# Column sums of two norms as one sum of two blocks, split into high and low parts, against one sum in fp32 of each block

## The chip, the core and the metric

The kernel runs on one core of one Trainium2 chip. Four engines compute: TensorE (PE) multiplies matrices, and its weight loads are listed as PEld; VectorE (DVE) and ScalarE (ACT) work element by element; GpSimd (POOL) and SyncE (SP) issue most of the transfers here. Every engine works through its own queue in order. SBUF holds 128 partitions; matrix products arrive in PSUM banks of 128 x 512 floats. The metric is the time of one execution on the device, in microseconds (us); lower is better.

## The reference: one step of a two-layer decoder

1024 prompt tokens and 8 sample tokens of width 2048 pass through layer A (an input projection, causal pooling over windows of 2 to 16 tokens, a linear map for each group, a SiLU gate, an output projection), then through layer B (sliding-window attention over a key and value computed once, a gate, an output projection). After each layer stands the same residual and norm:

```python
def layer_norm(x, g, b):
    xf = x.astype(jnp.float32)
    mu = jnp.mean(xf, axis=-1, keepdims=True)
    var = jnp.mean(jnp.square(xf - mu), axis=-1, keepdims=True)
    return ((xf - mu) * lax.rsqrt(var + LN_EPS) * g.astype(jnp.float32) + b.astype(jnp.float32)).astype(x.dtype)
...
    return layer_norm(ALPHA * x + y, g_ln, b_ln), new_state
```

All inputs and outputs are fp32.

## The kernel before

**Tiles.** Activations lie with the 2048 channels on the partitions: 16 tiles of 128 channels, handled two at a time as eight pairs p = 0..7, and the tokens along the row. The tokens come in two chunks: c = 0 with 512, and c = 1 with 520 (512 prompt tokens and the 8 samples). Most SBUF memory is a pool of 53 buffers of 128 x 1040 floats (`Mem`); `full()` takes a buffer, `half()` half of one, and what was freed longest ago is taken first.

**Products.** To hold fp32 accuracy in the faster form fp32r, every operand is split: ScalarE casts the high part (L473 for weights, L751 for activations), VectorE subtracts it from the whole to get the low part (L488, L760), and each product becomes three matmuls, high x high, high x low, low x high (L640 to L642, or L668 to L670 in the plain phases). Most projections go by Strassen's seven products of half blocks (`seven`, `pair`, `both`); PSUM is emptied by ScalarE and VectorE (L581 to L613).

**Steps.** The program is written out step by step: `begin()` loads, casts and splits weights some steps ahead (`ahead`), then 24 matmuls are issued, then `end()` raises the step counter `i` and issues what was put there with `at(n, go)` (n steps later) or, for TensorE, with `product(n, rank, go)`. Work beside the products is written as Python generators; `end()` advances the first of them one turn (up to its next `yield`) in every `every`-th step, if enough buffers are free. `in_order` then fixes the source order on TensorE, VectorE and ScalarE. The phases are ai (input projection A), ao (output projection A), bi and bo (the same of layer B), each for c = 0 and then c = 1.

**Norms.** A sum over channels is a sum over partitions and tiles. Pairs are first added up on VectorE into one buffer `acc` of two blocks (128 x 2 x T); the two blocks are then multiplied by J, a 128 x 128 matrix of 1/2048, which sums the partitions and puts the mean on each of them. That is `j_sum`: two fp32 matmuls that add up in one PSUM bank, for 520 tokens in two halves of 260 (L845). It is called
- in `shifted` (L1203), in the output phases of c = 0 (ao, bo) and in the last phase, bo of c = 1: the sum of the first pair gives a shift that is subtracted from every pair (L1217), so that the sums of squares (L1223, L1229) stay small. The step order for the first pair is: sum one step after, subtraction, squares and addition two, three and four steps after;
- in `ln_gen` (L864), a generator: the mean (L886), then for c = 0 the variance from the collected squares (L913), for c = 1 from squares of the centred values (L900; L914); then 1/sqrt (`rstd`, L856 to L859); then pair by pair the subtraction of the mean (L935), the multiplication (L936), scale and shift on ScalarE (L927) and the transfer out. `quiet()` yields until the PSUM bank of these sums (`psO`) has been unused for a step.

`ln_gen` runs three times: layer A, c = 0 during ao of c = 1 (a turn every second step); layer A, c = 1 during the first, plain part of bi of c = 0, with the transform of h behind it (`t_gen`); layer B, c = 0 during bo of c = 1 (a turn every third step; the rest is run out after the last product). The 520 tokens of layer B are normed by `phase_end`, which ends the program and has its own fp32 sums (L1291, L1367), untouched by the change. There the last three pairs are worked off with `less` (L1267), `rest` (L1273), `square` (L1278), `add` (L1281, L1282), `affine` (L1309, L1310, L1317), `scale` (L1329), then `moments` (L1383 to L1393) and the closing transposes and products (L1412, L1401, L1420) and evictions (L1432, L1437).

Of the kernel before, what the change touches and what calls it, by code (L numbers as in the profile page):

```python
# [10 lines left out]
F32R = mybir.dt.float32r  # L11
# [5 lines left out]
P = 128  # L17
D = 2048
NK = D // P
# [13 lines left out]
TMAX = 520  # L33
# [13 lines left out]
K_ID, K_MP, K_J, K_RC = 0, 128, 256, 384  # L47
# [134 lines left out]
class Kern:  # L182
    def __init__(self, ctx, tc, io):
        self.tc, self.io = tc, io
        self.nc = tc.nc
        pool = lambda name, **kw: ctx.enter_context(tc.tile_pool(name=name, **kw))
        one = pool("one", bufs=1)
        self.smp = pool("smp", bufs=2)
        dram = pool("dram", bufs=1, space=bass.MemoryType.DRAM)
        self.psd = [pool(f"psd{i}", bufs=1, space=bass.MemoryType.PSUM) for i in range(3)]  # L190
        self.pso = pool("pso", bufs=1, space=bass.MemoryType.PSUM)
        self.four = None
        ctx.callback(self.use_four, None)
        self.prm = one.tile([P, N_PRM], F32, name="prm")
        self.cst = one.tile([P, N_CST], F32, name="cst")
        self.mki = one.tile([P, P], I32, name="mki")
        self.nsink = one.tile([P, NH], F32, name="nsink")
        self.carry = one.tile([P, NK, NST], F32, name="carry")
        self.kdec = one.tile([P, 2, NDEC], F32, name="kdec")
        self.qd = [one.tile([P, NDEC, 8], F32, name=f"qd{i}") for i in range(2)]  # L200
        self.sgd = [one.tile([P, 8, NDEC], F32, name=f"sgd{i}") for i in range(2)]
        self.mem = Mem(pool("mem", bufs=1), NSLOT)
        self.n = 0
        self.i = self.e = self.lastO = self.turns = self.ring = 0
        self.posts, self.events, self.side = [], {}, []
# [12 lines left out]
        self.gbd = dram.tile([32, 2 * P], F32, tag="gbd", name="gbd")  # L218
        self.ws = {
            n: [dr(f"s{n}{q}", [P, 4, 1024]) for q in range(np_)]  # L220
            for n, np_ in (("wia", 16), ("woa", 8), ("wkv", 2), ("wib", 16), ("wob", 8))
        }
# [609 lines left out]
            yield  # L832


    def j_sum(self, T, src, out):

        J = self.cst[:, K_J : K_J + P]
        for s in [slice(0, T)] if T <= 512 else [slice(0, T // 2), slice(T // 2, T)]:
            n = s.stop - s.start
            if s.start == 0:  # L840
                ps = self.psO()[:, :n]
            else:
                ps = self.psW()[:, :n]
            for i, a in enumerate(src):
                self.nc.tensor.matmul(ps, J, a[:, s], start=i == 0, stop=i == len(src) - 1)  # L845
            out(s, ps)
# [17 lines left out]
    def ln_gen(self, c, pre, acc, gc, bc, out, td):  # L864
# [15 lines left out]
        flat = lambda s: s.a[:, : 2 * T]  # L880
        a2 = self.pair_view(acc, T)
        load(0)
        yield
        yield from self.quiet()
        load(1)
        self.j_sum(T, [a2[:, 0], a2[:, 1]], lambda s, ps: nc.scalar.copy(mu[:, s], ps))  # L886
        acc.free()
        yield
        w = self.mem.full()
        q, v = w.a[:, :T], w.a[:, TMAX : TMAX + T]  # L890
        if c == 0:
            sq = self.l_sq[0]
            nc.vector.tensor_mul(q, mu, mu)
        else:
            sq, sqs = self.mem.full(), {}
            for p in range(10):
                load(p + 2)
                if p < 8:
                    t = self.pair_view(pre[p], T)
                    nc.vector.tensor_sub(t, t, b2(mu))  # L900
                if 1 <= p <= 8:
                    sqs[p - 1] = sq if p == 1 else self.mem.full()
                    nc.scalar.activation(flat(sqs[p - 1]), flat(pre[p - 1]), AF.Square)
                yield
                if p > 2:
                    nc.vector.tensor_add(flat(sq), flat(sq), flat(sqs[p - 2]))
                    sqs[p - 2].free()
                yield
        s2 = self.pair_view(sq, T)
        yield from self.quiet()  # L910
        self.j_sum(
            T, [s2[:, 0], s2[:, 1]],
            lambda s, ps: nc.vector.scalar_tensor_tensor(v[:, s], ps, EPS, q[:, s], op0=ALU.add, op1=ALU.subtract)  # L913
            if c == 0 else nc.vector.tensor_scalar(v[:, s], ps, EPS, None, op0=ALU.add),  # L914
        )
        sq.free()
        yield
        self.rstd(v, rr, q)
        w.free()
# [283 lines left out]
    def shifted(self, c, p, s, pre, acc, end):  # L1203

        nc = self.nc
        T = CHUNKS[c][1]
        flat = lambda s: s.a[:, : 2 * T]
        box = {}

        def mean():  # L1210
            self.l_sq[c], self.l_sh[c] = self.mem.full(), self.mem.half()
            t = self.pair_view(s, T)
            self.j_sum(T, [t[:, 0], t[:, 1]], lambda h, ps: nc.scalar.mul(self.l_sh[c].a[:, h], ps, NK / 2.0))

        def less():
            t = self.pair_view(s, T)
            nc.vector.tensor_sub(t, t, self.l_sh[c].a[:, None, :T].to_broadcast([P, 2, T]))  # L1217
            if p >= KEEP0:
                nc.gpsimd.dma_start(self.act["p", c][:, 2 * p : 2 * p + 2, :], t)

        def square():
            q = box["q"] = self.l_sq[c] if p == 0 else self.mem.full()
            nc.scalar.activation(flat(q), flat(s), AF.Square)  # L1223

        def add():
            if p == 0:
                return
            nc.vector.tensor_add(flat(acc), flat(pre[0] if p == 1 else acc), flat(s))
            nc.vector.tensor_add(flat(self.l_sq[c]), flat(self.l_sq[c]), flat(box["q"]))  # L1229
            box["q"].free()  # L1230
            if p >= KEEP0:
                s.free(True)
            if p == 7:
                self.l_sh[c].free()

        if p == 0:
            pre.append(s)
            self.product(1, 1, mean)
        for n, go in zip((2, 3, 4) if p == 0 else (0, 1, 2), (less, square, add)):
            self.at(n, go)  # L1240

    def phase_end(self, c, xs, x_in, pre, acc, gc, bc, out):
# [761 lines left out]
    def start(self):  # L2004
# [19 lines left out]
        for j in range(4):  # L2024
            self.at(3 + 3 * j, lambda j=j: self.t_first(j))
        self.at(13, lambda: setattr(self, "x0", None))
        nc.vector.tensor_scalar(
            self.nsink[:], self.prm[:, C_SINK : C_SINK + NH], -1.0, None, op0=ALU.mult
        )
# [231 lines left out]
```

## Time and profile before

| | us |
|---|---|
| median of 3 runs | 2372.48 |
| lowest, highest | 2372.2, 2375.47 |
| the profiled execution | 2371.61 |
| its span, first to last instruction | 2369.8 |
| mean granted TensorE clock | 0.997 |

A row of the groups reads: line, engine, operation, output <- inputs (buffer numbers left out), shape, count | busy time, mean ns of one | idle time of the engine just before, and what ended it. In a timeline a row starts with its start and its duration in us; `x4` are four equal instructions in a row, and the bracket at the end is the idle time before it and what released it. TensorE's durations are longer than the distance from one start to the next, since matmuls are pipelined. An fp32 matmul leaves two records.

### The profile page before, as it was taken

How to read it: one execution, taken by the hardware profiler on the slowest of the kernel's cores; microseconds unless marked ns; L12 is line 12 of the kernel's file. 1: busy time of each engine (PE TensorE's matmuls, PEld its weight loads, DVE VectorE, ACT ScalarE, POOL GpSimd, SP SyncE). 2: the span in 40 equal slices, each digit the busy share in tenths (PEclk: the TensorE clock that was granted, in tenths of full speed). 3: DMA queues.
4: the chain of work that ended last, by engine and by line, in shares of the span. 5: the costliest groups of instructions: out<-in, count | busy, mean ns of one | idle time of the engine just before them, and what ended most of it. 6: DMA issues, size and time to landing. Idle time of an engine off the chain costs nothing. (4 is left out here: it accounts for less than half of the span.)

```text
span 2369.8 us, 46551 instructions
## 1 busy us (share of the span) xinstructions
PE 2335.5 (99%) x18444; PEld 2224.0 (94%) x18444; DVE 1914.7 (81%) x2369; ACT 1338.8 (56%) x2420; POOL 203.1 (9%) x379
## 2 busy tenths in 40 slices
PE   8999999999999999999999999999999999999998
PEld 6899999999999999998878899999999999999997
DVE  8787988776778878958988888887777768888787
ACT  4444446544546447644554666685666668546556
POOL 0111110011000000000111111100000000000001
PEclk9999999999999999999999999999999999999999
DMA  8678879989889979989888766788777768699785
GB/s 293 214 247 302 281 285 349 321 294 325 275 306 340 321 270 331 324 309 326 304 317 316 258 216 227 254 286 277 239 243 226 225 192 297 222 355 370 263 316 178
DMA packets 252059, 669.18 MB, mean 282 GB/s; under 512 B 25760, under 2 KB 106560, under 8 KB 251840
## 3 DMA queue, kind: packets, MB, share of 16 engines
q1 hardware_dynamic: 206368, 501.14, 63.2%
q0 software_dynamic: 45472, 165.07, 17.8%
q8 instruction: 144, 2.36, 0.4%
q14 instruction: 75, 0.61, 0.1%
HBM read 471.01 MB, written 185.59 MB: 277 GB/s over the span
## 5 line engine op out<-in xcount | busy, mean ns | idle before, releaser
L640 PE MATMUL pD<-m,m 128*128 128x260 f32 (+1 forms) x4752 | 1349.4, 284 | 9.8 <-DVE m L601 5.6
L642 PE MATMUL pD<-m,m 128*128 128x260 f32 (+1 forms) x4752 | 1340.8, 282 | 3.2 <-DVE m L488 3.2
L641 PE MATMUL pD<-m,m 128*128 128x260 f32 (+1 forms) x4752 | 1340.2, 282 | 0.0
L640 PEld LDWEIGHTS pD<-m,m 128*128 128x128 f32 x4752 | 896.0, 189 | 21.9 <-issue 12.9
L642 PEld LDWEIGHTS pD<-m,m 128*128 128x128 f32 x4752 | 896.7, 189 | 4.6 <-DVE m L488 4.4
L641 PEld LDWEIGHTS pD<-m,m 128*128 128x128 f32 x4752 | 896.6, 189 | 1.7 <-issue 1.4
L488 DVE TENSOR_TENSOR m<-m,m 128x1024 fp32r<-128x1024 f32 x674 | 814.5, 1219 | 101.7 <-ACT m L473 63.2
L473 ACT CAST m<-m 128x1024 fp32r<-128x1024 f32 x674 | 701.7, 1048 | 299.6 <-DVE m L331 72.6
L668 PE MATMUL pD<-m,m 128*128 128x512 f32 x448 | 179.7, 401 | 8.0 <-ACT m L751 8.0
L669 PE MATMUL pD<-m,m 128*128 128x512 f32 x448 | 177.2, 396 | 0.7 <-DVE m L760 0.7
L670 PE MATMUL pD<-m,m 128*128 128x512 f32 x448 | 177.2, 395 | 0.0
L760 DVE TENSOR_TENSOR m<-m,m 128x1024 fp32r<-128x1024 f32 (+1 forms) x120 | 147.0, 1226 | 6.6 <-ACT m L751 5.0
L613 ACT COPY m<-pD 128x260 f32<-128x260 f32 (+1 forms) x83 | 31.1, 375 | 195.2 <-PE pD L642 194.7
L751 ACT CAST m<-m 128x1024 fp32r<-128x1024 f32 (+1 forms) x120 | 125.8, 1052 | 13.6 <-PE pD L669 5.2
L331 DVE TENSOR_TENSOR m<-m,m 128x1024 f32<-128x1024 f32 x88 | 107.6, 1222 | 6.7 <-DMA m<-in_wia 3.8
L668 PEld LDWEIGHTS pD<-m,m 128*128 128x128 f32 x448 | 84.7, 189 | 29.9 <-ACT m L751 8.0
L601 DVE TENSOR_TENSOR m<-pD,m 128x260 f32<-128x260 f32 (+1 forms) x86 | 36.5, 424 | 85.7 <-PE pD L642 85.5
L669 PEld LDWEIGHTS pD<-m,m 128*128 128x128 f32 x448 | 84.7, 189 | 20.6 <-DVE m L760 1.8
L670 PEld LDWEIGHTS pD<-m,m 128*128 128x128 f32 x448 | 84.6, 189 | 19.7
L1729 ACT ACTIVATE m<-m,sm 128x128 f32<-128x128 f32 x256 | 99.4, 392 | 0.0
L1024 PE MATMUL pD<-m,m 128*128 128x260 f32 (+1 forms) x528 | 91.5, 323 | 0.0
L1024 PEld LDWEIGHTS pD<-m,m 128*128 128x128 f32 x528 | 79.5, 188 | 8.2
(235 smaller groups left out, 2125.0 us busy)
## 6 DMA issues: line engine op xcount, KB each, us to landing
m<-in_wia SPq DMA_DIRECT2D x124, 512.0 KB
m<-in_wib SPq DMA_DIRECT2D x120, 512.0 KB
swia<-m POOLq DMA_DIRECT2D x64, 512.0 KB, 4.6
m<-swia SPq DMA_DIRECT2D x64, 512.0 KB
m<-swoa SPq DMA_DIRECT2D x64, 512.0 KB
swib<-m POOLq DMA_DIRECT2D x64, 512.0 KB, 5.5
m<-swib SPq DMA_DIRECT2D x64, 512.0 KB
m<-swob SPq DMA_DIRECT2D x56, 512.0 KB
```

Source lines behind the costliest of these rows:

```text
L331: self.nc.vector.tensor_add(s[out].a[:, :1024], s[x].a[:, :1024], s[y].a[:, :1024])
L473: self.nc.scalar.copy(hi.r[:, :1024], self.stream[self.cast].src().a[:, :1024])
L488: self.nc.vector.tensor_sub(lo.r[:, :1024], s.src().a[:, :1024], hi.a[:, :1024])
L640: nc.tensor.matmul(ps[:, :TH], wh[:, s], h, start=new and k == 0, stop=False, skip_group_check=on)
L641: nc.tensor.matmul(ps[:, :TH], wh[:, s], l, start=False, stop=False, skip_group_check=on)
L642: nc.tensor.matmul(ps[:, :TH], wl[:, s], h, start=False, stop=k == 7, skip_group_check=on)
L668: nc.tensor.matmul(ps[:], wh[:, s], h, start=par == 0 and k == 0, stop=False)
L669: nc.tensor.matmul(ps[:], wh[:, s], l, start=False, stop=False)
L670: nc.tensor.matmul(ps[:], wl[:, s], h, start=False, stop=par == 1 and k == 7)
L751: self.nc.scalar.copy(h.r[:, :n], s.a[:, :n])
L760: self.nc.vector.tensor_sub(l.r[:, :n], s.a[:, :n], h.a[:, :n])
L1024: nc.tensor.matmul(ps[:, : cs.stop - cs.start], ws[:, s], d[:, cs], start=f0 and k == 0, stop=l0 and k == 3,)
```

## The change

`j_sum` is given one sum in two parts instead of two blocks. `j_steps` makes them in three steps: VectorE adds the two blocks (`add`), ScalarE casts the sum to fp32r (`high`), VectorE subtracts (`low`). J is cast to fp32r once, in the ninth step of the program (`jr`). The two matmuls of each sum are then fp32r. In `shifted` the three steps are put at the steps 0, 1 and 2 behind the first pair and the sum at 3 instead of 1; the work of the first two pairs moves two steps back. In `ln_gen` for c = 0 the three steps of the mean and of the variance are done together, in three turns at the start, where one yield stood; for c = 1 the three steps of the variance come one turn each ahead of its sum, and the mean stays as it was, in fp32 (`j_sum32`).

```diff
+        self.jr = one.tile([P, P], F32R, name="jr")
...
+    def j_steps(self, T, a, b, box, *free):
+
+        def add():
+            box["u"] = self.mem.half()
+            self.nc.vector.tensor_add(box["u"].a[:, :T], a, b)
+            for f in free:
+                f.free()
+
+        def high():
+            box["hl"] = self.mem.full()
+            self.nc.scalar.copy(box["hl"].r[:, :T], box["u"].a[:, :T])
+
+        def low():
+            u, hl = box.pop("u"), box["hl"]
+            self.nc.vector.tensor_sub(hl.r[:, TMAX : TMAX + T], u.a[:, :T], hl.a[:, :T])
+            u.free()
+
+        return add, high, low
+
+    def j_sum(self, T, box, out):
+
+        J, hl = self.jr[:], box.pop("hl")
+        src = hl.r[:, :T], hl.r[:, TMAX : TMAX + T]
...
+        hl.free()
+
+    def j_sum32(self, T, src, out):
+
+        J = self.cst[:, K_J : K_J + P]
...
     def ln_gen(self, c, pre, acc, gc, bc, out, td):
...
         load(0)
-        yield
+        mean, var = {}, {}
+        put = lambda s, ps: nc.scalar.copy(mu[:, s], ps)
+        if c == 0:
+            s2 = self.pair_view(self.l_sq[0], T)
+            steps = (
+                self.j_steps(T, a2[:, 0], a2[:, 1], mean, acc), self.j_steps(T, s2[:, 0], s2[:, 1], var, self.l_sq[0])
+            )
+            for k in range(3):
+                for st in steps:
+                    st[k]()
+                yield
+        else:
+            yield
         yield from self.quiet()
         load(1)
-        self.j_sum(T, [a2[:, 0], a2[:, 1]], lambda s, ps: nc.scalar.copy(mu[:, s], ps))
-        acc.free()
+        if c == 0:
+            self.j_sum(T, mean, put)
+        else:
+            self.j_sum32(T, [a2[:, 0], a2[:, 1]], put)
+            acc.free()
...
-        s2 = self.pair_view(sq, T)
+            s2 = self.pair_view(sq, T)
+            for go in self.j_steps(T, s2[:, 0], s2[:, 1], var, sq):
+                go()
+                yield
...
     def shifted(self, c, p, s, pre, acc, end):
...
         if p == 0:
             pre.append(s)
-            self.product(1, 1, mean)
-        for n, go in zip((2, 3, 4) if p == 0 else (0, 1, 2), (less, square, add)):
+            t = self.pair_view(s, T)
+            for n, go in enumerate(self.j_steps(T, t[:, 0], t[:, 1], box)):
+                self.at(n, go)
+            self.product(3, 1, mean)
+        for n, go in zip({0: (4, 5, 6), 1: (2, 3, 4)}.get(p, (0, 1, 2)), (less, square, add)):
             self.at(n, go)
...
+        self.at(9, lambda: nc.scalar.copy(self.jr[:], self.cst[:, K_J : K_J + P]))
```

More of the change, by code (lines that the diff above doesn't have):

```diff
@@ L832, in t_gen @@
             yield
-    def j_sum(self, T, src, out):
-        J = self.cst[:, K_J : K_J + P]
+    def j_steps(self, T, a, b, box, *free):
[15 more added lines that the diff above has]
+        src = hl.r[:, :T], hl.r[:, TMAX : TMAX + T]
         for s in [slice(0, T)] if T <= 512 else [slice(0, T // 2), slice(T // 2, T)]:
@@ L843, in j_sum @@
                 ps = self.psW()[:, :n]
+            for i, a in enumerate(src):
+                self.nc.tensor.matmul(ps, J, a[:, s], start=i == 0, stop=i == len(src) - 1)
+            out(s, ps)
+        hl.free()
+    def j_sum32(self, T, src, out):
+        J = self.cst[:, K_J : K_J + P]
+        for s in [slice(0, T)] if T <= 512 else [slice(0, T // 2), slice(T // 2, T)]:
+            ps = (self.psO() if s.start == 0 else self.psW())[:, : s.stop - s.start]
             for i, a in enumerate(src):
@@ L891, in ln_gen @@
         if c == 0:
-            sq = self.l_sq[0]
             nc.vector.tensor_mul(q, mu, mu)
@@ L908, in ln_gen @@
                 yield
-        s2 = self.pair_view(sq, T)
+            s2 = self.pair_view(sq, T)
+            for go in self.j_steps(T, s2[:, 0], s2[:, 1], var, sq):
+                go()
+                yield
         yield from self.quiet()
         self.j_sum(
-            T, [s2[:, 0], s2[:, 1]],
+            T, var,
             lambda s, ps: nc.vector.scalar_tensor_tensor(v[:, s], ps, EPS, q[:, s], op0=ALU.add, op1=ALU.subtract)
@@ L915, in ln_gen @@
         )
-        sq.free()
         yield
@@ L1211, in mean @@
             self.l_sq[c], self.l_sh[c] = self.mem.full(), self.mem.half()
-            t = self.pair_view(s, T)
-            self.j_sum(T, [t[:, 0], t[:, 1]], lambda h, ps: nc.scalar.mul(self.l_sh[c].a[:, h], ps, NK / 2.0))
+            self.j_sum(T, box, lambda h, ps: nc.scalar.mul(self.l_sh[c].a[:, h], ps, NK / 2.0))
         def less():
```

## The prediction

> **What bounds the kernel now.** I read the page's engine table first, then TensorE's waits, then the timeline at each column sum, and last the chain that ended last.
>
> ```profile
> span 2369.8 us, 46551 instructions
> PE 2335.5 (99%) x18444; PEld 2224.0 (94%) x18444; DVE 1914.7 (81%) x2369; ACT 1338.8 (56%) x2420; POOL 203.1 (9%) x379
> ...
> L473 ACT CAST m<-m 128x1024 fp32r<-128x1024 f32 x674 | 701.7, 1048 | 299.6 <-DVE m L331 72.6
> ```
> ```profile
> PE pD L640 <- DVE m L601: 5.6, 5, 2.6
> ...
> PE pD L642 <- DVE m L488: 3.2, 5, 0.9
> ```
>
> TensorE runs through; its waits for VectorE (DVE) are 5.6 us for a bank freed late (L601) and 3.2 us for a weight split late (L488). So what leaves TensorE's queue shortens the kernel, unless VectorE, at 81%, is the limit just there. The windows tell where that is (columns: length; busy time of PE, PEld, DVE, ACT, POOL; clock; DMA share; GB/s):
>
> ```profile
> 2040.00:2085.00 45.00, 42.90 (x383) 40.66 (x382) 40.03 (x46) 21.73 (x32) 5.91 (x11) 1.00 0.84 297
> 2160.00:2200.00 40.00, 37.38 (x298) 35.78 (x297) 39.68 (x37) 29.46 (x39) 1.07 (x2) 1.00 1.03 376
> 2300.00:2337.00 37.00, 37.00 (x298) 36.53 (x297) 28.31 (x38) 22.40 (x37) 2.84 (x4) 1.00 0.61 201
> 2337.00:2352.00 15.00, 15.00 (x117) 14.59 (x116) 14.73 (x24) 10.36 (x23) 3.60 (x5) 1.00 0.28 101
> ```
>
> TensorE loses 2.1 us in 2040 to 2085 and 2.6 in 2160 to 2200, both at the start of an output phase. In the end (2337 to 2352) VectorE has 0.3 us free.
>
> **Removed: column sums in fp32.** TensorE's timeline at one 512-token sum and at the two halves of a 520-token one:
>
> ```profile
> 802.20 1.88 PE L845 MATMUL pO<-m,cst 128*128 128x512 f32 x4
> ...
> 804.03 0.28 PE L641 MATMUL pD<-m,m 128*128 128x256 f32 x1
> ...
> 1091.26 0.40 PE L669 MATMUL pD<-m,m 128*128 128x512 f32 x1
> 1091.49 0.40 PE L670 MATMUL pD<-m,m 128*128 128x512 f32 x1
> 1091.73 1.04 PE L845 MATMUL pO<-m,cst 128*128 128x260 f32 x4
> ...
> 1093.71 0.39 PE L669 MATMUL pD<-m,m 128*128 128x512 f32 x1
> ```
> ```profile
> 2329.13 0.28 PE L640 MATMUL pD<-m,m 128*128 128x260 f32 x1
> 2329.25 0.28 PE L641 MATMUL pD<-m,m 128*128 128x260 f32 x1
> ```
>
> Durations overlap, so starts count. From the sum's start to that of the second matmul behind it are 1.83 us; a 256-column matmul takes 0.12, so the sum cost 1.71. The new one is two fp32r matmuls of 512 columns: 0.23 from start to start at L669/L670, so 0.46; 1.25 saved. For 520 tokens: 1093.71 less 1091.73 less 0.23 is 1.75, against four at 0.12, 0.48: 1.27 saved. Six sums of 512 change (two shifts; mean and variance of two norms) and two of 520 (a variance, the last shift); the 520-token mean stays. 6 x 1.25 + 2 x 1.27 = **10.0 us off TensorE**.
>
> **Added: eight adds, eight subtractions, eight casts, one cast of J.** On VectorE a subtraction of this size, and what the sums make it wait for:
>
> ```profile
> 2308.47 0.69 DVE L1281 TENSOR_TENSOR m<-m,m 128x520 f32<-128x520 f32 x1
> 2309.08 0.69 DVE L1282 TENSOR_TENSOR m<-m,m 128x520 f32<-128x520 f32 x1
> ...
> 947.96 0.69 DVE L913 SCALAR_TENSOR_TENSOR m<-pO,m 128x512 f32<-128x512 f32 x1 [3.37 <-PE pO L845]
> ...
> 2050.65 1.22 DVE L488 TENSOR_TENSOR m<-m,m 128x1024 fp32r<-128x1024 f32 x1
> ...
> 2054.20 1.23 DVE L1217 TENSOR_TENSOR m<-m,m 128x1024 f32<-128x1024 f32 x1 [1.75 <-ACT m L1213]
> ...
> 2209.83 0.69 DVE L913 SCALAR_TENSOR_TENSOR m<-pO,m 128x512 f32<-128x512 f32 x1 [2.40 <-PE pO L845]
> ...
> 2226.42 1.24 DVE L1217 TENSOR_TENSOR m<-m,m 128x1040 f32<-128x1040 f32 x1 [2.26 <-ACT m L1213]
> ```
>
> From start to start 0.61, so 1.2 us for each sum, 10 in all; the casts take about half of the 1.05 that ACT needs for 1024 elements (L473), and ACT is 56% busy: nothing. Each step waits for the one before: ACT's cast for the add, with the weight casts queued behind it, VectorE's subtraction for the cast, with the weight splits behind, TensorE's sum for the subtraction, with all products behind. With a step (24 x 0.12, 2.9 us) or a turn between them, each is done before it is asked for. In the layer-A norm of 512 tokens 2.4 us go in ahead of an idle of 3.37; in the layer-B one ahead of 2.40: nothing there. What covers VectorE's lateness elsewhere is that weights are prepared ahead; without that cover each sum would pay its 1.2.
>
> At 2051 the cover is thin. The split at 2050.65 ends at 2051.87; today TensorE is in the column sum meanwhile. With the sum two steps later and an add ahead of that split, TensorE asks at about 2051.8 and gets it at 2052.5: it waits 0.7. Behind, the shift's subtraction (L1217), with the weight splits queued behind it, no longer stands 1.75 us ahead of two of them, which returns some. Bounds for this stage: a gain of 0.5 to a loss of 2.5 (TensorE's gain and VectorE's add both lost); I take a **loss of 0.6**, nearest to the 0.7 just worked out.
>
> **Moved: the norm of the 512 tokens comes later.** Adding, casting and subtracting are three turns of the norm's generator where one yield was: two turns more. In layer A that is four steps, and it still ends six steps before the next phase asks for it. Each turn's load on SyncE (512 KB) and its output move with it, past weight loads; with the DMA engines 0.61 busy in 2300 to 2337 that costs nothing. In layer B a turn comes every third step and only with five free buffers, and today the generator is done just before the loop ends. In the changed program's instruction order two of the eight subtract/multiply pairs (L935, L936) move in behind the last of today's: one pair behind the L1273 at 2323.25, one behind L859; the two double affines (L927) of the last two tile pairs go to ACT behind today's second L1329 group and between the tail's later L1329 and L1278. The ends of those queues now:
>
> ```profile
> 2314.63 1.22 DVE L935 TENSOR_TENSOR m<-m,m 128x1024 f32<-128x1024 f32 x1
> ...
> 2317.03 1.22 DVE L488 TENSOR_TENSOR m<-m,m 128x1024 fp32r<-128x1024 f32 x1
> ...
> 2323.25 0.69 DVE L1273 TENSOR_TENSOR m<-m,m 128x520 f32<-128x520 f32 x1
> ...
> 2335.76 0.43 DVE L859 SCALAR_TENSOR_TENSOR m<-m,m 128x260 f32<-128x260 f32 x1
> 2336.77 0.43 DVE L611 TENSOR_TENSOR m<-pD,m 128x260 f32<-128x260 f32 x1 [0.58 <-PE pD L642]
> ```
> ```profile
> 2314.84 1.53 ACT L927 ACTIVATE m<-m,prm 128x512 f32<-128x512 f32 x2
> 2316.27 0.36 ACT L587 COPY m<-pD 128x260 f32<-128x260 f32 x1
> ...
> 2345.70 1.10 ACT L1317 ACTIVATE m<-m,prm 128x260 f32<-128x260 f32 x2 [2.74 <-DVE m L1310]
> ...
> 2353.03 0.36 ACT L1383 COPY m<-pD 128x260 f32<-128x260 f32 x1
> ```
>
> The first pair fits in VectorE's 8.7 free microseconds of 2300 to 2337. The second takes 2.40 (2314.63 to 2317.03) from 2336.1, so L611 starts at 2338.5, 1.75 later than at 2336.77. From there to 2352 VectorE does not idle, ACT waits for it at 2345.70, and ACT runs through from there to L1383, which opens the last norm's chain: 1.75 late. The second L927 double adds 1.43 (2314.84 to 2316.27) inside that run: L1383 is **3.2 us later** against TensorE's last products. Bounds: nothing, if the cover is larger than I read, to 7.7 (two pairs and two doubles, all in series). The last output transfer of that norm, issued then, has 15 us until the end and costs nothing. The DMA queues gain no transfer.
>
> One rule of the Trainium skill bears on this tail: "TensorE: Matmul & The Clock Gate" (Part 1, the HAM clock gate) says that about 3.4 us of idleness halve the array's clock. This case's clock:
>
> ```profile
> 2350.00:2355.00 5.00, 4.76 (x32) 4.15 (x30) 2.88 (x6) 4.25 (x12) 0.00 (x0) 1.00 0.31 107
> 2355.00:2360.00 5.00, 2.75 (x8) 2.08 (x9) 4.77 (x10) 3.35 (x8) 0.00 (x0) 0.81 0.15 53
> ```
> ```profile
> 2347.91 0.28 PE L642 MATMUL pD<-m,m 128*128 128x260 f32 x1
> 2348.03 1.04 PE L1412 MATMUL pD<-cst,m 128*128 128x128 f32 x8
> ...
> 2356.29 0.44 PE L1401 MATMUL pD<-cst,m 128*128 128x128 f32 x2 [1.53 <-DVE m L1391]
> ```
>
> The trace agrees: the clock drops only where TensorE begins to wait. By that rule the longer wait would send the twenty transposes behind the last column sums through at half speed, an estimated 2 us more (they take 0.1 each), 1.5 of them inside today's idle before L1401; the sum would be 0.5 later.
>
> **Sum.** The profiled execution took 2371.61 (span 2369.8 and 1.8 around it): 2371.61 - 10.0 + 0.6 + 3.2 = 2365.4. The median of the runs, 2372.48, is 0.9 above that execution: **2366.3**.
>
> **Rivals.**
> 1. *The tail hides it.* The moved pairs run in VectorE's idle time and ACT's 2.74 at 2345.70. For it: 8.7 us free just before. Against: order is fixed, and the second pair stands behind L859. Then 2372.48 - 10.0 = 2362.5.
> 2. *VectorE takes it back.* TensorE's gains come where VectorE fills 40.03 of 45 and 39.68 of 40 us; the four sums in or just behind these windows (the two layer-B shifts, mean and variance) lose their 1.25: 2366.3 + 4 x 1.25 less the 0.6 already in, 2370.7. Against: VectorE itself idles 2.40 and 2.26 us at two of the four.
> 3. *A late transformed block starves the second layer's start* (slower). The 520-token norm ends later, so the h transform behind it ends four steps (2.8 us each) later; SyncE, in order, would wait with its load of it, and weight loads queue behind that load. If none of the four steps is slack, 11.2 us: 2366.3 + 11.2 = 2377.5; it decides from about 6 us on. TensorE's one long wait there:
>
> ```profile
> 1367.74 0.36 PE L640 MATMUL pD<-m,m 128*128 128x256 f32 x1 [2.62 <-DVE m L601]
> ```
>
> For it: the place is tight. Against: that wait is for VectorE, not for a transfer.
> 4. *The sums get no cheaper*, the fp32r form of J costing what fp32 does: 2366.3 + 10.0 = 2376.3. Against: the rows L669/L670 are this very form.
>
> **How the numbers follow.** Forecast 0.54, rival 1 0.17, rival 2 0.18, rival 3 0.08, rival 4 0.03. About 0.2%, 4.7 us, is what a measurement here tells from no change, so faster means under 2367.7. The forecast's own range is 2364 to 2369, four fifths of it below that line: 0.43 and 0.11; rival 1 is faster, rival 2 the same, 3 and 4 slower. Faster 0.60, same 0.29, slower 0.11. The range takes in rivals 1 and 2 with their bounds: 2361 to 2371.5.
>
> **What would show it.** The new sums' rows: two records of about 0.4 us, start to start 0.23, for each 512 sum. TensorE's wait for L488 near 2051: 0.7. The last L935/L936 behind L859, with L611 some 2.4 us behind it. From the last product to L1383, now 2353.03 less 2347.91, 5.1 us: about 8.3. Wrong, if that distance stays, if TensorE's idle time at the phase starts grows by more than 2 us, or if the second layer's start shows a wait for a load.

## The result and the profile after

| | before | after |
|---|---|---|
| median of 9 runs each, us | 2373.51 | 2367.30 |
| lowest to highest | 2371.83 to 2375.47 | 2366.07 to 2368.44 |
| the profiled execution | 2371.61 | 2367.62 |
| its span | 2369.8 | 2365.9 |

The ratio is 0.9979 (95% interval 0.9970 to 0.9988): faster by 6.2 us in the medians. The two profiled executions lie 4.0 apart; before's was 1.9 under the median of its runs, after's 0.3 over. Lines behind `j_steps` have moved: the sums' L845 is L866 now (L876 for the mean left in fp32), L488 is L489, L601 L602, L611 L612, L859 L890, L913 and L914 are L961 and L962, L935 and L936 L982 and L983, L927 L974, L1278 L1327, L1329 L1378, L1383 L1432, L1412 L1461, L1367 L1416, L1401 L1450; the products' L640 to L642 and L668 to L670 are one line further down. L840, L846 and L850 are the new add, cast and subtraction.

The page and TensorE's waits of the changed kernel:

```profile
span 2365.9 us, 46542 instructions
PE 2326.4 (98%) x18424; PEld 2219.4 (94%) x18424; DVE 1923.5 (81%) x2385; ACT 1342.2 (57%) x2429; POOL 201.5 (9%) x379
```
```profile
PE pD L643 <- DVE m L489: 4.5, 7, 1.4
PE pD L641 <- DVE m L602: 3.7, 4, 1.4
...
PE pD L641 <- ACT m L1778: 2.6, 1, 2.6
PE pD L1450 <- DVE m L1440: 1.9, 1, 1.9
PE pS L1742 <- DVE m L1714: 1.5, 1, 1.5
PE pD L1461 <- DVE m L595: 1.0, 1, 1.0
```

TensorE is 9.1 us less busy (2335.5 to 2326.4), but the span shrank by 3.9: it waits more, for weight splits (L489: 3.2 before, 4.5 now), once at L1742, and in the last norm (L1461, L1450, and 0.9 at L1416), though less for banks freed late (L602: 5.6 before, 3.7 now). Its timeline shows the sums themselves:

```profile
807.48 0.62 PE L866 MATMUL pO<-m,jr 128*128 128x512 f32 x2
807.94 0.28 PE L641 MATMUL pD<-m,m 128*128 128x256 f32 x1
...
1146.02 0.40 PE L866 MATMUL pO<-m,jr 128*128 128x260 f32 x2
1146.26 0.40 PE L866 MATMUL pD<-m,jr 128*128 128x260 f32 x2
1146.50 0.40 PE L669 MATMUL pD<-m,m 128*128 128x512 f32 x1
```

A 512-token sum takes 0.46 us from its start to that of the product behind it, a 520-token one 0.48: the prices of the prediction.

Every product is the same matmul in the same place of TensorE's order in both kernels, so the two traces can be laid side by side. Start of the same product matmul, in us:

| place | before | after | after less before |
|---|---|---|---|
| ahead of the first sum | 365.23 | 364.85 | -0.4 |
| behind layer A's shift | 809.62 | 807.94 | -1.7 |
| behind mean and variance, layer A, 512 | 971.17 | 967.13 | -4.0 |
| behind the variance of 520 | 1151.79 | 1146.50 | -5.3 |
| behind L1742's wait | 1163.00 | 1159.25 | -3.8 |
| still so, 500 us on | 1663.62 | 1659.84 | -3.8 |
| behind layer B's first shift (bo, c = 0) | 2076.39 | 2072.53 | -3.9 |
| start of bo, c = 1, over | 2177.22 | 2172.57 | -4.7 |
| behind layer B's mean, variance and last shift | 2231.55 | 2223.17 | -8.4 |
| the next pair of blocks | 2240.93 | 2233.35 | -7.6 |
| last product | 2347.91 | 2340.52 | -7.4 |
| end of the span | 2369.8 | 2365.9 | -3.9 |

Outside bo of c = 0 the sums brought 1.3, 2.4, 1.2 and 3.7 us. Five places gave back or gained: 1.5 us at 1159, the whole sum at the start of bo (c = 0), 0.8 gained by 2177, 0.8 lost behind 2223, 3.5 lost behind the last product.

**The tail.** VectorE, ScalarE and TensorE behind the last products of the changed kernel:

```profile
2328.59 0.43 DVE L890 SCALAR_TENSOR_TENSOR m<-m,m 128x260 f32<-128x260 f32 x1
2328.93 1.22 DVE L982 TENSOR_TENSOR m<-m,m 128x1024 f32<-128x1024 f32 x1
2330.19 1.22 DVE L983 TENSOR_TENSOR m<-m,m 128x1024 f32<-128x1024 f32 x1
2331.33 0.42 DVE L612 TENSOR_TENSOR m<-pD,m 128x260 f32<-128x260 f32 x1
```
```profile
2343.58 0.90 ACT L1378 ACTIVATE m<-m,prm 128x256 f32<-128x256 f32 x2
2344.38 1.51 ACT L974 ACTIVATE m<-m,prm 128x512 f32<-128x512 f32 x2
2345.79 0.40 ACT L1327 ACTIVATE m<-m 128x260 f32<-128x260 f32 x1
...
2349.00 0.35 ACT L1432 COPY m<-pD 128x260 f32<-128x260 f32 x1
```
```profile
2340.52 0.28 PE L643 MATMUL pD<-m,m 128*128 128x260 f32 x1
2340.64 0.63 PE L1461 MATMUL pD<-cst,m 128*128 128x128 f32 x4
2342.30 0.66 PE L1461 MATMUL pD<-cst,m 128*128 128x128 f32 x4 [1.02 <-DVE m L595]
...
2346.25 1.58 PE L1416 MATMUL pD<-m,cst 128*128 128x260 f32 x6 [0.88 <-ACT m L1327]
```

The moved pair stands between L890 and L612, which starts 2.74 us behind L890 (1.01 before); the moved double affine (L974) stands inside ScalarE's closing run and takes 1.41 of it. From the last product to L1432 are 8.5 us (2349.00 less 2340.52), against 5.1 before. TensorE does not wait in one piece but in two short ones, ahead of the transposes and in the last sums.

**VectorE in layer A's norm of 520 tokens:**

```profile
1139.97 0.70 DVE L850 TENSOR_TENSOR m<-m,m 128x520 fp32r<-128x520 f32 x1 [1.00 <-ACT m L846]
...
1146.46 0.43 DVE L962 TENSOR_SCALAR m<-pO 128x260 f32<-128x260 f32 x1 [3.85 <-PE pO L866]
...
1158.41 0.69 DVE L1714 TENSOR_TENSOR m<-m,m 128x512 f32<-128x512 f32 x1
```

VectorE stands 1.00 behind the cast and 3.85 behind the sum, 4.8 us in all. Its read of the sum is queued ahead of everything else, and what follows includes the first attention block's preparation: L1714 ends at 1159.1, and TensorE, which starts its part at 1159.25, waited 1.5 us for it. In the kernel before, the reads of the same sum cost VectorE 0.93 and 0.45:

```profile
1142.77 0.43 DVE L914 TENSOR_SCALAR m<-pO 128x260 f32<-128x260 f32 x1 [0.93 <-PE pO L845]
1143.65 0.43 DVE L914 TENSOR_SCALAR m<-pD 128x260 f32<-128x260 f32 x1 [0.45 <-PE pD L845]
```

**VectorE at the start of bo, c = 0:** the windows of the changed kernel, with the same columns as before (the second is the start of bo, c = 1):

```profile
2036.00:2081.00 45.00, 41.81 (x381) 40.36 (x381) 41.37 (x48) 21.83 (x32) 5.90 (x11) 1.00 0.84 287
...
2156.00:2196.00 40.00, 37.77 (x312) 37.12 (x311) 40.00 (x38) 31.04 (x40) 1.06 (x2) 1.00 1.02 369
```

In the first, VectorE works 1.3 us more than before (41.37 against 40.03) and TensorE loses 1.1 more (41.81 busy against 42.90). TensorE's waits for splits there, in the changed kernel and in the one before:

```profile
PE pD L643 <- DVE m L489: 2.5, 4, 1.4
```
```profile
PE pD L642 <- DVE m L488: 1.4, 3, 0.6
```

A wait of 0.46 at 2048.8 is new, one is 0.25 at 2065.3 instead of 0.55, and one is 1.35 at 2072.5 instead of 0.42: 1.1 us more in all.

### The profile page after: what moved, and what is told of

It reads as the page before. It is cut to its first block, busy times and chain, and to the rows that moved or that the text cites. A ratio compares the mean times of both kernels' runs of the same rounds, so it can differ in the third digit from the quotient of the medians.

```text
span 2365.9 us, 46542 instructions
## 1 busy us (share of the span) xinstructions
PE 2326.4 (98%) x18424; PEld 2219.4 (94%) x18424; DVE 1923.5 (81%) x2385; ACT 1342.2 (57%) x2429; POOL 201.5 (9%) x379
## 5 line engine op out<-in xcount | busy, mean ns | idle before, releaser
L642 PE MATMUL pD<-m,m 128*128 128x260 f32 (+1 forms) x4752 | 1340.3, 282 | 0.0
L641 PEld LDWEIGHTS pD<-m,m 128*128 128x128 f32 x4752 | 896.0, 189 | 21.0 <-issue 10.2
L643 PEld LDWEIGHTS pD<-m,m 128*128 128x128 f32 x4752 | 896.7, 189 | 6.0 <-DVE m L489 6.0
L642 PEld LDWEIGHTS pD<-m,m 128*128 128x128 f32 x4752 | 896.3, 189 | 0.5
L489 DVE TENSOR_TENSOR m<-m,m 128x1024 fp32r<-128x1024 f32 x674 | 814.1, 1219 | 96.1 <-ACT m L474 58.3
L670 PE MATMUL pD<-m,m 128*128 128x512 f32 x448 | 177.2, 396 | 0.5 <-DVE m L761 0.5
L669 PEld LDWEIGHTS pD<-m,m 128*128 128x128 f32 x448 | 84.7, 189 | 29.9 <-ACT m L752 8.0
L670 PEld LDWEIGHTS pD<-m,m 128*128 128x128 f32 x448 | 84.8, 189 | 20.4 <-DVE m L761 1.6
L671 PEld LDWEIGHTS pD<-m,m 128*128 128x128 f32 x448 | 84.6, 189 | 19.8
L602 DVE TENSOR_TENSOR m<-pD,m 128x260 f32<-128x260 f32 (+1 forms) x86 | 36.4, 424 | 81.9 <-PE pD L643 78.6
L607 DVE TENSOR_TENSOR m<-pD,m 128x260 f32<-128x260 f32 (+1 forms) x84 | 35.6, 424 | 64.2 <-PE pD L643 64.0
```

The source lines that it names most:

```text
L489: self.nc.vector.tensor_sub(lo.r[:, :1024], s.src().a[:, :1024], hi.a[:, :1024])
L641: nc.tensor.matmul(ps[:, :TH], wh[:, s], h, start=new and k == 0, stop=False, skip_group_check=on)
L642: nc.tensor.matmul(ps[:, :TH], wh[:, s], l, start=False, stop=False, skip_group_check=on)
L643: nc.tensor.matmul(ps[:, :TH], wl[:, s], h, start=False, stop=k == 7, skip_group_check=on)
L669: nc.tensor.matmul(ps[:], wh[:, s], h, start=par == 0 and k == 0, stop=False)
L670: nc.tensor.matmul(ps[:], wh[:, s], l, start=False, stop=False)
```

## The experiments

Each time stands beside the ratio to the kernel before, measured on the same chip at the same time; the positions are start times of the same product matmul, as in the table above. What counts is by how much a distance between two traces changes at a place, not how large it is, because the traces differ ahead of every edit. The window 361 to 366 of the changed kernel and of version 4, whose edit lies far behind it:

```profile
361.00:366.00 5.00, 5.00 (x31) 5.00 (x31) 4.97 (x5) 3.52 (x6) 0.53 (x1) 0.66 1.02 378
```
```profile
361.00:366.00 5.00, 4.73 (x40) 4.74 (x41) 4.97 (x6) 4.88 (x8) 0.53 (x1) 1.00 1.05 365
```

The granted clock was 0.66 in the profiled executions of both kernels and 1.00 in those of versions 1, 4, 5, 6 (fp32), 8 and 9, which therefore stand 0.9 to 1.4 us ahead of the changed kernel from 366 on. The same happens at 1364 to 1372, where only versions 10 and 11 keep the full clock and gain 1.5 and 1.2.

**1. The price of the sums.** The changed kernel with its two products in fp32.

```diff
-        J, hl = self.jr[:], box.pop("hl")
-        src = hl.r[:, :T], hl.r[:, TMAX : TMAX + T]
+        J, hl = self.cst[:, K_J : K_J + P], box.pop("hl")
+        src = hl.a[:, :T], hl.a[:, TMAX : TMAX + T]
```

> The changed kernel with every added step, but the sums' two matmuls are fp32 again (J and both parts read as fp32). Theory: the products' 10.0 us come back, less some 2.5 where VectorE is the limit (the plain attention part and the start of the last output phase of the first 512 tokens), so 7.5 to 10 us slower than the changed kernel: 2375 to 2377, ratio to before 1.0005 to 1.0015; each 512 sum takes 1.71 us again. Rival (the gain comes from the moved order, not from the products): about as fast as the changed kernel, 2367 to 2369.

2378.41, ratio 1.0024 (1.0014 to 1.0035): 11.1 us over the changed kernel. In the trace the two stand level behind the first sum (808.0), and the last product lies 10.4 later: each of the seven other sums brings 1.25 to 1.3, two longer waits, at 919 and 2155, 1.0 and 0.6. The 2.5 that the expectation took off, because VectorE was held to be the limit at two of the sums, were not saved: at 1146 and 2055 the sums cost 1.27 and 1.25 like the others. The whole gain is the cheaper form, and the adds, casts and subtractions alone, without it, make a kernel slower than before.

**2. The tail, from the other side.** The kernel before with two empty turns ahead of layer B's norm of 512 tokens; the sums stay in fp32.

```diff
         yield
+        if c == 0 and gc == C_GB:
+            yield
+            yield
```

> The kernel before, with two empty turns ahead of the layer-B norm of 512 tokens and nothing else of the change. Theory: the late norm alone costs the tail 3.2 to 3.7 us: 2376.9, ratio 1.0014; TensorE's timeline is that of before up to 2300 us. Rival (the tail lost its time to the sums or their casts): no difference, ratio 1.0000.

2375.49, ratio 1.0012 (1.0003 to 1.0021). The timeline of this version, TensorE's last product and ScalarE's first copy of the last sums:

```profile
2348.34 0.28 PE L642 MATMUL pD<-m,m 128*128 128x260 f32 x1
```
```profile
2356.86 0.35 ACT L1386 COPY m<-pD 128x260 f32<-128x260 f32 x1
```

8.5 us lie between the two, as in the changed kernel. So the tail's loss has nothing to do with the form of the sums; the two turns alone make it.

**3. No extra turns in layer B's norm,** by doing the three steps of mean and variance in one turn.

```diff
             for k in range(3):
                 for st in steps:
                     st[k]()
-                yield
+                if gc != C_GB or k == 2:
+                    yield
```

> The changed kernel, but the layer-B norm of 512 tokens does its three preparing steps in one turn instead of three, so that it ends as early as before the change. Theory (the late norm costs 3.2 us in the tail; the trace of the changed kernel lost 3.7 there): about 3.5 us faster than the changed kernel, 2363.8, and from the last product to the copy that opens the closing moments 5 us, as before the change. Rival (the tail hides it, what was lost lies elsewhere): the same as the changed kernel, 2367.3. Against before: ratio 0.9960 or 0.9975.

2367.85, ratio 0.9981 (0.9972 to 0.9990): no gain. The tail is back to 5.1 us (2345.33 to 2350.41), but 4.3 went between 2150 and 2207, of which 1.0 comes back by 2221, since this version's two sums stand earlier. ScalarE and TensorE there:

```profile
2190.25 1.22 ACT L846 CAST m<-m 128x512 fp32r<-128x512 f32 x2 [2.99 <-DVE m L840]
2191.37 0.37 ACT L597 COPY m<-pD 128x260 f32<-128x260 f32 x1
```
```profile
2191.79 0.39 PE L641 MATMUL pD<-m,m 128*128 128x260 f32 x1 [2.11 <-ACT m L597]
```

ScalarE's cast (L846) waits 2.99 us for VectorE's add; behind the cast stands an eviction (L597), and TensorE waits 2.11 for that. This is the case that the distance of a turn was there to avoid.

**4. One turn, but a step between the three parts.**

```diff
+            if gc == C_GB:
+                for st in steps:
+                    st[0]()
+                    self.at(0, st[1])
+                    self.at(1, st[2])
+                yield
-            for k in range(3):
+            for k in range(0 if gc == C_GB else 3):
```

> The changed kernel (2367.3), but in the layer-B norm of the 512 tokens the three preparing steps use one turn: the adds in the turn, the casts one step later, the subtractions two steps later, the sum in the next turn, three steps later. Theory: the tail's 3.5 us come from the two extra turns alone, and the 5.3 us that the version with everything in one turn lost came from ScalarE standing at its casts behind VectorE's adds with evictions behind. So the tail's 3.5 come back, and at most the 1.2 us of the subtractions are lost between 2157 and 2200, where VectorE never idles: 2364.5 (2363.8 to 2365.0). Rival: any work that comes into that full stretch earlier costs what it takes there, and the gain is lost again: 2367 or more.

2365.26, ratio 0.9973 (0.9962 to 0.9983). Last product and copy:

```profile
2341.27 0.28 PE L643 MATMUL pD<-m,m 128*128 128x260 f32 x1
```
```profile
2346.44 0.36 ACT L1438 COPY m<-pD 128x260 f32<-128x260 f32 x1
```

The tail is 5.2 us. Between 2150 and 2202 this version loses 1.8 against the changed kernel, of which 0.9 come back by 2220 (the two sums stand earlier). The span is 2.4 shorter, 2.1 of it gained behind 2150; the median is 2.0 below the changed kernel's, from another set of runs. The intervals of the two ratios overlap, so the trace carries this and not the times.

**5. Layer B's norm with both sums as before.**

```diff
-        if c == 0:
+        if c == 0 and gc != C_GB:
             s2 = self.pair_view(self.l_sq[0], T)
...
-        if c == 0:
+        if c == 0 and gc != C_GB:
             self.j_sum(T, mean, put)
...
+        if c == 0 and gc == C_GB:
+            s2 = self.pair_view(self.l_sq[0], T)
+            var = [s2[:, 0], s2[:, 1]]
-        self.j_sum(
+        (self.j_sum32 if c == 0 and gc == C_GB else self.j_sum)(
             T, var,
```

> The changed kernel, but the layer-B norm of the 512 tokens has both its sums in fp32 as before, and no extra turns. Theory: two sums give back 1.25 us each, the tail's 3.5 go, and the 0.8 us longer wait at 2233 goes: 2367.3 + 2.5 - 3.5 - 0.8 = 2365.5; so for this norm the change loses more than it gains. Rival: the tail's loss has nothing to do with this norm's turns: 2369.8.

2367.66, ratio 0.9982 (0.9973 to 0.9991), 2.2 above the theory. The tail is 5.1 us, and the two sums give back 1.3 each; but the wait at 2233 did not go (1.71, against 1.38 in the changed kernel), and 1.0 and 0.6 were lost at 2155 and 2173, ahead of any of this norm's sums, in waits for ScalarE whose cause was not looked for. The sums' 2.5 stand against the tail's 3.4; with these losses the version is not told apart from the changed kernel (medians 0.4 apart).

**6. The 520-token variance in one turn, and in fp32.** Two versions, one with the three steps in one turn, one with the fp32 sum and no extra turns:

```diff
             for go in self.j_steps(T, s2[:, 0], s2[:, 1], var, sq):
                 go()
-                yield
+            yield
```
```diff
-            for go in self.j_steps(T, s2[:, 0], s2[:, 1], var, sq):
-                go()
-                yield
...
-        self.j_sum(
-            T, var,
+        (self.j_sum if c == 0 else self.j_sum32)(
+            T, var if c == 0 else [s2[:, 0], s2[:, 1]],
```

> The changed kernel, but the variance of the 520-token norm in layer A does its add, cast and subtraction in one turn with the sum one turn later, two turns earlier than in the changed kernel. Theory (VectorE stood 3.85 us behind this late sum, and the rotation of the queries behind it came 1.5 us late for TensorE): TensorE's wait of 1.5 us at 1157 us goes, the kernel is about 1.5 us faster, 2365.8. Rival (the added VectorE work itself makes it late): the wait stays above 1 us, the time is the same, 2367.3.

> The changed kernel, but the variance of the 520 tokens in layer A is summed in fp32 as before, with no extra turns. Theory: TensorE's wait of 1.5 us at 1159 goes, the sum costs 1.27 more: 2367.1, with TensorE at 1250 some 0.2 earlier than in the changed kernel. Rival, from the version with these steps in one turn: turns that shift hand out other buffers, and a load nearly a millisecond later (the transposed o at 2130) comes late by up to 6 us: 2371 to 2373, with that wait at that place.

2373.36, ratio 1.0005 (0.9996 to 1.0015), and 2372.72, ratio 1.0007 (0.9998 to 1.0016). In both TensorE's wait at 1159 went. In the one-turn version it came again at 1183 (1.3 us), and a wait for ScalarE at 1544 grew by 1.0; in the fp32 version it stayed away. That version stands 0.93 ahead of the changed kernel before this sum, for the clock's sake, and 1.09 ahead at 1260: 0.2 gained, as the theory had it, so the fp32r sum with its two turns is worth nothing here. But nearly a millisecond later both lost 5.8 and 4.5 us at 2135, in bo of c = 0, where nothing had been touched.

**7. The shift of bo, c = 0, as before** (fp32 at its old steps).

```diff
+        box, old = {}, (self.ph, c) == ("bo0", 0)
...
+            (self.j_sum32 if old else self.j_sum)(T, [t[:, 0], t[:, 1]] if old else box, lambda h, ps: nc.scalar.mul(self.l_sh[c].a[:, h], ps, NK / 2.0))
...
-            for n, go in enumerate(self.j_steps(T, t[:, 0], t[:, 1], box)):
+            for n, go in enumerate(() if old else self.j_steps(T, t[:, 0], t[:, 1], box)):
...
-            self.product(3, 1, mean)
+            self.product(1 if old else 3, 1, mean)
+        w = {0: (2, 3, 4)} if old else {0: (4, 5, 6), 1: (2, 3, 4)}
```

> The changed kernel, but the shift's sum in the output phase of layer B, 512 tokens, is fp32 and at its old steps. Theory: VectorE is the limit in 2040 to 2085, so that the change gained nothing there: TensorE's position at 2100 stays within 0.3 us of the changed kernel's, 2367.3 plus or minus 0.3. Rival: the sum's 1.25 us count there and the losses have another cause: 2368.6.

2373.99, ratio 1.0009 (0.9999 to 1.0018). From 2040 to 2073 it lost 0.1 against the changed kernel (0.91 to 1.05 behind it), as the theory had it for this place: of the sum's 1.25 the change kept no more than that. Then the same place at 2135 took 5.9. VectorE and SyncE of this version:

```profile
2138.06 0.43 DVE L809 TENSOR_TENSOR m<-m 128x260 f32<-128x260 f32 x1 [6.10 <-DMA m<-o]
```
```profile
2118.14 0.69 SPq L822 DMA_DIRECT2D m<-o  x1
2120.41 0.33 SPq L273 DMA_DIRECT2D m<-in_wob  x1
2121.64 2.84 SPq L273 DMA_DIRECT2D m<-swob  x2
2129.51 0.33 SPq L273 DMA_DIRECT2D m<-in_wob  x1
2129.94 0.39 SPq L1204 DMA_DIRECT2D m<-h  x1
2130.42 0.39 SPq L822 DMA_DIRECT2D m<-o  x1
```

What SyncE waits for in 2119 to 2140 of this version, and SyncE of the changed kernel at the same place:

```profile
SPq L273 <- DMA to<-m: 4.9, 1, 4.9
```

```profile
2117.14 3.01 SPq L822 DMA_DIRECT2D m<-o  x2
2120.32 0.33 SPq L273 DMA_DIRECT2D m<-in_wob  x1
2120.75 2.73 SPq L273 DMA_DIRECT2D m<-swob  x2
```

The transform of o takes its loads from L822. In the changed kernel the last two are issued together, ahead of the weight loads. Here the last one stands behind the weight load at 2129.51, which waits 4.9 us until its buffer, the last holder of a block of the transformed o (`to`), has been written out. `in_order` fixes the order on three engines only; SyncE's is left to the scheduler. That it places a load by when it expects the buffer to be free, and that the edits changed which buffer that is, is a likely reason, not a shown one. Between 2110 and 2140 the order of SyncE's transfers is that of the changed kernel in versions 1 to 5 and that of this one in all three that lost at 2135. Behind TensorE's wait of 5.8 us there the clock was 0.50 in 2142 to 2146, which cost 2.6 more; by 2172 3.0 had come back, because TensorE then waits less at the start of bo, c = 1.

**8. The same, with the transform of o three steps earlier.**

```diff
-                self.at(18, lambda: add(("o", 1, False), self.t_gen(("o", 1))))
+                self.at(15, lambda: add(("o", 1, False), self.t_gen(("o", 1))))
```

> The version with the fp32 shift in the output phase of layer B (2373.99), and the generator that transforms o starts three steps earlier there, so that its last load is issued ahead of the weight load that waits for an outgoing transfer. Theory: nearly all that that version lost (7.4 us in the trace, 6 of them in one stall at 2135 to 2143) is this late load; with it gone the stall of VectorE at the first subtraction of the transform goes, and the time is 2367 to 2368.5. Rival: the fp32 sum itself or its step order starves the phase: the stall stays, 2372 to 2374.

2367.28, ratio 0.9979 (0.9968 to 0.9989): the product that started at 2141.95 starts at 2135.32. Of these 6.6 us, 1.7 stand there already at 2040, 1.1 were lost at 2081, where the transform's work now lies, and the stall itself (5.8 us of waiting) is gone. The late load it was.

**9. Versions 4, 6 (fp32) and 8's early transform together.**

> Three edits on the changed kernel: the layer-B norm's three preparing steps in one turn, a step apart (2365.26 by itself); the 520-token variance of layer A in fp32; the transform of o three steps earlier. Theory, by adding up: the variance's fp32 sum gives back 1.3 and takes 1.8 of waits away (0.5 faster by the trace of the version that has it alone), and the late load of o that made that version 5 us slower is gone: 2364.8, or 2364 to 2366. Rival: the late load is not what made it slower: 2370 or more.

2362.02, ratio 0.9957 (0.9945 to 0.9970), faster than both kernels: its slowest run, 2365.52, is under the changed kernel's fastest, 2366.07. The median is 2.8 below the sum of the parts, but that sum (ratio 0.9969) still lies within the interval. Its window at the start of bo, c = 1:

```profile
2155.00:2195.00 40.00, 39.68 (x329) 39.20 (x328) 40.00 (x39) 31.37 (x42) 0.53 (x1) 1.00 1.02 370
```

TensorE loses 0.3 of 40 us there, against 2.2 in the changed kernel. Versions 8 and 10, the others with the early transform, gain there too in their traces (1.3 and 2.4 between 2150 and 2186, this one 2.9), which was not in the theory. The 0.5 that the theory takes from the trace of version 6 (fp32) is the 0.2 said there.

**10. The early transform alone, in the kernel before,** to see whether that gain has to do with the sums.

> The kernel before, with the transform of o three steps earlier and nothing else. Theory: the version with all three edits gained 2.4 us at 2155 to 2173 over the one without the last two, because the transform's work and loads leave the start of the last output phase earlier; that has nothing to do with the sums, so before gains 1.5 to 2.5 too: 2370 to 2371. Rival: this gain exists only together with the new step order: 2372.2, no change.

2371.92, ratio 1.0001 (0.9992 to 1.0010). The profiled execution (span 2367.4) is 2.4 us shorter than that of the kernel before, but 1.5 of it lie at 1368 to 1372, where its clock stayed full. Then it loses 1.1 at 2085, where the transform's work now lies, and gains 2.5 by 2182: 1.4 in the trace, nothing in the medians. What the early transform is worth by itself stays open within 2 us.

**11. The shift from the high parts alone,** on top of version 4: one cast of both blocks, no add, no subtraction, the sum one step earlier.

```diff
+        def high():
+            box["hl"] = self.mem.full()
+            nc.scalar.copy(
+                box["hl"].r.rearrange("p (k t) -> p k t", k=2)[:, :, :T], self.pair_view(s, T)
+            )
...
-            self.product(3, 1, mean)
+            self.at(0, high)
+            self.product(2, 1, mean)
```

> The version with the layer-B norm's preparing steps a step apart (2365.26), and in the three output phases the shift is summed from the high parts of the first pair's two blocks alone: one cast of both blocks on ScalarE, then two fp32r matmuls, the sum at the second step instead of the third. This changes which number is used as the shift (a rounded mean); the same number is subtracted everywhere. VectorE loses an add and a subtraction (1.2 us) for each of three shifts, ScalarE's casts become twice as long (0.5 us more). Theory: at 2047 to 2085 and 2210 to 2235 VectorE is the limit, so about 1 us comes back at the first and 0.5 to 1 at the second: 2363.5 (2363 to 2364.5). Rival: what limits there is the order of steps and the weights' arrival, not VectorE's time: 2365.3, no change.

2366.22, ratio 0.9975 (0.9965 to 0.9985), not told apart from version 4. In the trace 1.0 us is gained between 2048 and 2072, as the theory had it, and 2.5 lost again at 2231 to 2236, where TensorE waits 2.4 for the eviction L602 (1.4 in the changed kernel) and the clock behind that wait is 0.74 in 2231 to 2235. So at the first place VectorE's time counted, and TensorE's too, since version 1 lost its 1.25 there. At the second the cause is open: this version's shift has neither the add nor the subtraction, and the wait is longer still.

## Why the prediction was right, and where not

The forecast was 2366.3 (2361.0 to 2371.5), faster; the median is 2367.3. Its three terms, step by step:

- **Ten microseconds off TensorE: right.** The sums cost 0.46 and 0.48 as worked out; the seven outside bo of c = 0 brought 8.6 us against 5 x 1.25 + 2 x 1.27 = 8.8, and the version with fp32 products lost 11 (rival 4 falls).
- **The tail, +3.2: right, mechanism and size.** From the last product to L1432 8.5 us were measured, 8.3 forecast; L612 came 2.74 behind L890, 2.4 forecast. The two empty turns in the kernel before made the same 8.5, and every version without the turns 5.0 to 5.2. Rival 1 falls. The sentence on the clock did not come true: the windows

```profile
2346.00:2351.00 5.00, 3.99 (x26) 3.27 (x26) 1.51 (x4) 4.25 (x12) 0.00 (x0) 1.00 0.41 158
2351.00:2356.00 5.00, 2.80 (x11) 2.01 (x11) 4.77 (x10) 3.36 (x9) 0.00 (x0) 0.88 0.15 53
```

  show the twenty transposes (2347.66 to 2350.3) at full clock. What failed was the picture of one long wait: it came as 1.02 and 0.88. By the rule in the Trainium skill's "TensorE: Matmul & The Clock Gate" (Part 1, the HAM clock gate) a halving takes an idle of about 3.4 us. The two waits fit that, but other places do not, and there the measurement decides: the clock fell to half behind a wait of 1.94 (last section), and in the tail of the kernel before, where the prediction saw agreement, the longest single wait was 1.53.
- **The start of bo, c = 0, +0.6: right place, too small.** The traces give a loss of 1.2 of the sum's 1.25 (-3.8 ahead, -3.9 behind), the version with the old sum there 1.1; both lie within the bounds of -0.5 to 2.5. The error is in what was to follow the 0.7 at 2051, which came as 0.46: 0.3 returned at the next split, as forecast, but a later one, at 2072.5, took another 0.9, so that VectorE's 1.2 us of add and subtraction were nearly all paid.
- **Costs set to nothing elsewhere: wrong at one place.** That with a turn between the steps "each is done before it is asked for" failed in layer A's norm of 520 tokens, where a turn comes almost every step and other work stands in between: VectorE waited 1.00 for the cast and 3.85 for the sum, and TensorE 1.5 for what was queued behind that. The prediction had VectorE's idle time for the norms of 512 tokens only. Since the sum is worth 1.27, this edit gains nothing; the fp32 version stood 0.2 better.
- **Not foreseen at all:** 0.8 lost behind 2223, where the wait for the eviction L602 grew from 0.6 to 1.4. That three sums now start within 12 us there (2210.3 to 2222.7; 26 before) is not the reason: in version 2 they do so too and the wait is 0.17, and in versions 4 and 5, where they are spread over about 30 us, it is 1.7. Every version with the new last shift has at least 1.3 there, every one with the old at most 0.6; what in the shift's new steps makes it is open. And 0.8 gained by 2177, ahead of any sum of that phase: two waits for ScalarE, 0.7 each, became 0.3, for a reason that was not looked for.

Rival 2 was half true: the shift in bo, c = 0, was lost, the three sums in bo, c = 1, were not, but for 0.8 of their 3.7. Rival 3 did not come: TensorE's long wait at the start of the second layer's next part is 2.6 us as before and is put down to ScalarE, not to a load. A late load did decide the time of three experiments, but at 2135 and for another reason.

Against its own execution the sum made 2365.4, and 2367.6 was measured: 1.5 (variance of 520), 0.6 (bo), 0.8 (behind 2223), 0.3 (tail) and 0.2 (the sums) too little, less 0.8 (by 2177) and 0.4 (ahead of the first sum). So the two profiled executions lie 4.0 apart where the terms give 6.2; the medians do lie 6.2 apart (with the experiments, the median of the kernel before was 2371.1 to 2372.5, which would make it 3.8 to 5.2). The terms were too good by 2.2 in the traces, and before's profiled execution happened to lie 1.9 under its median, after's 0.3 over: that the two cancel, and that the forecast came within 1.0 of the median, is luck.

## What to carry to other kernels

Price a cheaper instruction by its start-to-start distance in the trace and look for it at once in every place where it is used, not at one of each kind: of eight like gains here six arrived and two were eaten by the engine that prepares their input. Before reading one trace against another, see whether they stand level ahead of the edit. Work that is done in turns pays for an added turn at its end; count how many turns are left before the last one, and put the parts of a step on neighbouring steps rather than on turns of their own. Where only some queues have a fixed order, compare the others' order of instructions before believing a difference of some microseconds: one load in another place cost about as much as the change under study brings.

## What the runs showed of the hardware that was not expected

TensorE's rows around the fall of the clock in the changed kernel:

```profile
2352.24 0.44 PE L1450 MATMUL pD<-cst,m 128*128 128x128 f32 x2 [1.90 <-DVE m L1440]
2353.64 1.17 PE L1469 MATMUL pD<-m,m 128*128 128x512 f32 x4 [0.96 <-issue]
```

The granted clock was 1.00 in 2346 to 2351 and 0.88 in 2351 to 2356, although the longest idle was 1.90 us: two short matmuls stand between it and the next of 0.96. A stretch of little work was enough.

One wait among dense products was enough too, but not in every execution. Behind a wait of 1.94 us that ends at 360.7 the changed kernel's clock was 0.50 in 362 to 364; behind 1.95 at the same place version 4 had 1.00. Behind 2.57 at 1364 the changed kernel had 0.50 in 1365 to 1368; behind 2.69 version 11 had 1.00. Each halving costs 1.2 to 1.5 us here, so profiled executions of one and the same code can lie that far apart.
